# Low parts of the mixer's weights: made once and kept in DRAM

## The chip, the core and the metric

The kernel runs on one core of a Trainium2 chip. Its engines work side by side, each with its own queue of instructions taken in order: TensorE (PE) multiplies, VectorE (DVE), ScalarE (ACT) and GpSimd (POOL) work element by element, SyncE (SP) issues the DMAs here. The metric is device time of one execution in microseconds (us), as the median of several runs; less is better.

## The reference

One decoder layer on x of 2048 tokens by 1024 channels, all float32: a mixer of two groups of gated linear attention heads, then a squared-ReLU MLP, each between RMS norms. Cut to what matters here:

```python
def hybrid_mixer(h, w_in, w_gk_up, b_gk, gla_norm_w, hgrn_norm_w, lb, w_out):
    z = h @ w_in                     # 1024 x 3600
    gq, gk, gv, gg, glr, hq, hf, hi, hg = jnp.split(z, _split_points(), axis=-1)
    ...
    o_a = gated_head_norm(chunked_gated_linear_attention(q_a, k_a, v_a, log_a), gg, gla_norm_w)
    ...
    o_b = gated_head_norm(chunked_gated_linear_attention(q_b, k_b, v_b, jnp.log(f)), hg, hgrn_norm_w)
    return jnp.concatenate([o_a, o_b], axis=-1) @ w_out       # 1024 x 1024

h = x + rmsnorm(hybrid_mixer(rmsnorm(x, pre_mix_norm), w_in, ...), post_mix_norm)
u = rmsnorm(h, pre_mlp_norm) @ w_up
out = h + rmsnorm(jnp.square(jax.nn.relu(u)) @ w_down, post_mlp_norm)
```

## The kernel before

PE multiplies in a rounded float32 format. To keep precision each operand is written as a high part (the value rounded to that format, made by ACT) and a low part (value minus high part, made by DVE or POOL), and each product is three matmuls: high by high, high by low, low by high (`mm3`, L236 to 241). `split` (L224) makes the pair: L229 is ACT's copy, L230 the subtraction.

The mixer runs over four blocks of 512 tokens (`mixer`, L299). A block goes through four units of heads in the order 0, 2, 3, 1 and then the output projection `out_proj` (L700). A unit projects its query, key or gate channels (`zchan`, L427; weights stationary) and then its values and output gates (`values`, L443; activations stationary, four token tiles against eight pieces of weight). Unit 0 has 16 columns more and takes each piece in two matmuls of 272 and 256 columns. The attention itself is made of tasks that are advanced between these products (`tile_task`, L526; decays L565, scores L632, states L654, outputs L687).

The weights come as pieces of 128 x 512 (128 x 528 for the values of unit 0). `plan` (L271) lists 72 pieces for each block, the same 72 four times: 56 of `w_in` and 16 of `w_out`. Each names the engine of its subtraction: POOL for the channel pieces and every second value piece (40 of 72), DVE for the rest (32). The class `Weights` (L39) handles them: `load` (L53) issues the DMAs of a piece on SP (L64; one for a channel or `w_out` piece, two for a value piece, three in unit 0) into one of 4 raw buffers `wr`, up to four pieces ahead of the last one split; `prep` (L69) splits one; `pump` (L82) splits up to n more while fewer than 12 are live; `take` hands one to the products, `free` counts those that the products are done with. High and low parts share 24 buffers `w`. A raw buffer is free again when the subtraction has read it. So every block loads and splits all weights anew.

SP also issues all other transfers: x and its transpose, the residuals of the block before (`residual`, L772; L790, L801), and in block 3 the operands of the MLP's first product (`combine`, L807): its operands are loaded (L819), scaled by ACT, added by POOL and stored (L824), 16 loads and 28 stores for its first half. After the mixer come `up` and `down`, the two MLP products, which the change leaves alone. The order of instructions on each engine is set when the program is built, by a scheduler that goes by priority and by its own estimate of when things are ready.

Of the kernel before, what the change touches and what calls it, by code (L numbers as in the profile page):

```python
# [7 lines left out]
F32 = mybir.dt.float32  # L8
F32R = mybir.dt.float32r
I32 = mybir.dt.int32  # L10
AF = mybir.ActivationFunctionType
# [5 lines left out]
P = 128  # L17
# [9 lines left out]
NG = FF // P // GF  # L27
WM = 528
WS = 576
NFLAG = P * (2 * NCH + 1)  # L30
EPS = 1e-6
LIMIT = 64.0
# [6 lines left out]
class Weights:  # L39

    LIVE = 12
    RAW = 4

    def __init__(self, layer):
        self.layer, self.plan, self.raw, self.parts = layer, [], {}, {}
        self.loaded = self.split = self.taken = self.freed = 0

    def add(self, views, chan=False, eng="vector"):  # L50
        self.plan.append((views, chan, eng))

    def load(self):  # L53
        y = self.layer
        while self.loaded < len(self.plan) and self.loaded < self.split + self.RAW:
            views, chan, _ = self.plan[self.loaded]
            raw = y.wp.tile([P, WM], F32, tag="wr", name=y.name("wr"), bufs=self.RAW)
            at = 0
            for v in views:
                n = v.shape[-1] * (4 if chan else 1)  # L60
                dst = raw[:, at:at + n]
                if chan:
                    dst = dst.rearrange("p (k n) -> p k n", n=P)
                y.nc.sync.dma_start(dst, v)  # L64
                at += n
            self.raw[self.loaded] = raw[:, :at]
            self.loaded += 1

    def prep(self):  # L69
        self.load()  # L70
        y, i = self.layer, self.split
        raw = self.raw.pop(i)
        n = raw.shape[-1]
        hi, lo = (y.wp.tile([P, WS], F32R, tag="w", name=y.name("w"), bufs=2 * self.LIVE)[:, :n] for _ in range(2))
        y.split(hi, lo, raw, eng=getattr(y.nc, self.plan[i][2]))
        if self.plan[i][1]:
            hi, lo = (z.rearrange("p (k n) -> p k n", n=P) for z in (hi, lo))
        self.parts[i] = (hi, lo)
        self.split += 1
        self.load()  # L80

    def pump(self, n):  # L82
        while n and self.split < len(self.plan) and self.split - self.freed < self.LIVE:
            self.prep()
            n -= 1

    def take(self):
        if self.split == self.taken:
            assert self.split - self.freed < self.LIVE
            self.prep()  # L90
# [7 lines left out]
class Layer:  # L98
# [21 lines left out]
        self.hold = False  # L120
        self.rs, self.hn, self.vdone, self.vg = {}, {}, {}, {}

    def run(self, h1d, h2d, hcd, ud):
        tc = self.tc
        self.h1d, self.h2d, self.hcd, self.ud = h1d, h2d, hcd, ud
        with tc.tile_pool(name=f"ac{self.tag}", bufs=1, reuse_waits="tile") as self.ac:


            with ExitStack() as late:
                with ExitStack() as ctx:  # L130
                    self.sb = ctx.enter_context(tc.tile_pool(name=f"sb{self.tag}", bufs=1))
                    self.ps = ctx.enter_context(tc.tile_pool(name=f"ps{self.tag}", bufs=1, space=PSUM))
                    with ExitStack() as early:
                        self.wp = early.enter_context(tc.tile_pool(name=f"wp{self.tag}", bufs=1, side="right"))
                        self.pz = early.enter_context(
                            tc.tile_pool(name=f"pz{self.tag}", bufs=1, space=PSUM, side="right"))
                        self.plan()
                        self.mixer()
                    self.open_up(late)
                    self.drain()  # L140
                    if not self.exact:
                        self.judge()
                self.up()
            self.down()
# [125 lines left out]

    def plan(self):  # L271
        io = self.io
        self.w = Weights(self)

        def chan(src, cols):
            for half in range(2):
                for col in cols:
                    rows = src[half * 512:half * 512 + 512, col:col + P]
                    self.w.add([rows.rearrange("(k p) n -> p k n", p=P)], True, "gpsimd")

        for b in range(NBLK):
            for u in self.UNITS:
                if u < 2:
                    chan(io["w_in"], (GQ + u * P, GK + u * P))
                else:
                    for h in (2 * u - 4, 2 * u - 3):
                        chan(io["w_in"], (HF + h * P,))
                        chan(io["w_in"], (HQ + h * P,))
                for k in range(KT):
                    self.w.add([io["w_in"][k * P:(k + 1) * P, c0:c0 + n] for c0, n in self.value_cols(u)],  # L290
                               eng=("gpsimd", "vector")[k % 2])
            for half in range(2):
                for u in self.UNITS:
                    for k in (2 * u, 2 * u + 1):
                        self.w.add([io["w_out"][k * P:(k + 1) * P, half * 512:half * 512 + 512]])
# [1 line left out]


    def mixer(self):  # L299
        for tag, n, width in (("wr", Weights.RAW, WM), ("w", 2 * Weights.LIVE, WS), ("pad", 1, 48)):  # L300
            self.wp.tile([P, width], F32R if tag == "w" else F32, tag=tag, name=self.name(tag), bufs=n)
        self.drain(self.stats(0))
        self.load_const("ident")
        self.pre_mix = self.static("pre_mix_norm", [P, KT])
        self.hn[0] = []
        for _ in self.prepare(0, 4):
            pass
        self.setup_mixer()
        for b in range(NBLK):
            self.b, self.oT, self.g = b, {}, {}  # L310
            if b == NBLK - 1:
                self.pre_mlp = self.small("pre_mlp", [P, KT])
                self.nc.sync.dma_start(self.pre_mlp, self.io["pre_mlp_norm"])

                def halves():
                    wide = [self.t([P, D], "wide") for _ in range(2)]
                    return [w[:, h * 512:h * 512 + 512] for w in wide for h in range(2)]

                self.spawn(self.combine(0, halves))
            for u in self.UNITS:  # L320
                if u == 3 and b + 1 < NBLK:
                    self.spawn(self.stats(b + 1))
                self.hold = True
                self.unit(u)
                self.hold = False
                self.step()
            self.out_proj(b)
# [479 lines left out]
    def combine(self, s, new):  # L807
# [5 lines left out]
        for j in range(4):  # L813
# [9 lines left out]
            def keep(i, tile):  # L823
                nc.sync.dma_start(self.hcd[i, s, j], tile)  # L824

            a21, a22 = load(j, 1), load(j + 4, 1)
            yield
            keep(3, a22)
# [426 lines left out]
def build(tc, io, force=False):  # L1255
    nc = tc.nc
    nc.scalar.preload_act_table_set("natural_log_exp_and_others")
    with ExitStack() as ctx:
        ent = ctx.enter_context
        cp = ent(tc.tile_pool(name="consts", bufs=1))  # L1260
        dp = ent(tc.tile_pool(name="scratch", bufs=1, space=DRAM))
        c = {}

        def const(key, shape, val):
            c[key] = cp.tile(shape, F32, name=f"c_{key}")
            nc.vector.memset(c[key], val)

        c["ident"] = cp.tile([P, P], F32, name="c_ident")
        c["cmask"] = cp.tile([P, P], I32, name="c_cmask")
        const("ones", [P, P], 1.0)  # L1270
        const("neghalf", [P, NCH], -0.5)
        const("flag_a", [P, NCH], 0.0)
        const("flag_b", [P, NCH], 0.0)
        const("fmin", [P, 1], 1.0)
        c["verdict"] = cp.tile([1, 1], I32, name="c_verdict")
        h1d = dp.tile([T, D], F32, name="h1_scratch")
        h2d = dp.tile([D, T], F32, name="h2_scratch")
        hcd = dp.tile([7, T // TM, 4, P, TB], F32, name="h2_operands")
        ud = dp.tile([7, T // TM, NG, P, TB], F32, name="u_operands")

        fast = Layer(tc, io, c, False)
        fast.run(h1d, h2d, hcd, ud)

        ok = nc.values_load(c["verdict"][0:1, 0:1], min_val=0, max_val=NFLAG)
        with tc.If(ok < (NFLAG + 1 if force else NFLAG)):
            slow = Layer(tc, io, c, True)
            slow.run(h1d, h2d, hcd, ud)


_OUT = "out"  # L1290
# [51 lines left out]
```

## Time and profile before

| | before |
|---|---|
| median of 3 runs | 2339.5 us (2334.85 to 2341.5) |
| the profiled execution | 2335.3 us |
| its span, first to last instruction | 2333.4 us |
| PE, DVE, ACT, POOL busy | 96%, 65%, 50%, 33% |
| mean granted clock of PE | 0.985 |
| bytes moved by DMA | 343 MB, 147 GB/s on average |

The profile is of one execution. "Busy" is the share of the span in which an engine works on an instruction; PE's matmuls overlap. The granted clock of PE has two levels, full (1.00, 2.4 GHz) and half (1.2 GHz). "DMA share" is the mean busy share of the 16 DMA engines. A wait is named by what ended it: "PE zp_f L240 <- DVE w_f L230" is PE, standing before a matmul of line 240, until DVE's instruction of line 230 had finished.

### The profile page before, as it was taken

The page shows a single profiled execution, that of the slowest core. Times are in us where ns is not written, and L with a number is a line of the kernel's source. Part 1 is how long each engine was busy: PE and PEld are TensorE (multiplying, and loading weights), DVE is VectorE, ACT ScalarE, POOL GpSimd, SP SyncE. Part 2 cuts the span into 40 slices and gives each one's busy share as a digit, 9 for nine tenths or more (in the row PEclk, how much of TensorE's full clock was granted, in tenths as well). Part 3 has the DMA queues.
Part 4 walks back from the last instruction along what each step waited for, and adds up shares of the span by engine and source line. Part 5 has one row for each costly group of instructions (what it writes and reads, how often), then busy time and mean ns, then how long its engine had stood idle before and what let it go on. Part 6 is the DMA issues. An engine that isn't in the chain of part 4 may idle for free. (4 is left out here: it accounts for less than half of the span.)

```text
span 2333.4 us, 31583 instructions
## 1 busy us (share of the span) xinstructions
PE 2241.2 (96%) x10922; PEld 1846.3 (79%) x10922; DVE 1517.6 (65%) x2368; ACT 1170.8 (50%) x2268; POOL 778.2 (33%) x537
## 2 busy tenths in 40 slices
PE   7999999999999889998999999999899999999995
PEld 6788878888788868876888878888788878888884
DVE  4675566555763676657775687655636776777687
ACT  5764566556654566455555565555543322333242
POOL 4330323124321543124532333333312332233265
PEclk9999999999999989999999999999999999999998
DMA  6322652246324752359744464444444433344265
GB/s 183 114 78 73 182 163 73 71 132 187 98 75 123 247 174 73 99 176 292 241 174 151 155 229 176 153 151 155 146 167 126 136 115 111 127 136 132 94 203 195
DMA packets 294762, 343.42 MB, mean 147 GB/s; under 512 B 25776, under 2 KB 214464, under 8 KB 294592
## 3 DMA queue, kind: packets, MB, share of 16 engines
q1 hardware_dynamic: 294592, 341.30, 45.5%
q8 instruction: 88, 1.44, 0.3%
q14 instruction: 82, 0.67, 0.1%
HBM read 242.65 MB, written 98.57 MB: 146 GB/s over the span
## 5 line engine op out<-in xcount | busy, mean ns | idle before, releaser
L239 PE MATMUL zp_f<-w_f,act_f 128*128 128x512 f32 (+2 forms) x896 | 329.8, 369 | 3.3 <-ACT ct_f L408 1.9
L240 PE MATMUL zp_f<-w_f,act_f 128*128 128x512 f32 (+2 forms) x896 | 326.0, 364 | 6.3 <-DVE w_f L230 4.5
L241 PE MATMUL zp_f<-w_f,act_f 128*128 128x512 f32 (+2 forms) x896 | 324.2, 364 | 0.0
L230 POOL TENSOR_TENSOR w_f<-wr_f,w_f 128x512 fp32r<-128x512 f32 (+1 forms) x160 | 220.8, 1391 | 285.0 <-ACT w_f L229 265.5
L868 ACT ACTIVATE u_f<-raw_f 128x1024 fp32r<-128x1024 f32 x111 | 117.7, 1061 | 332.3 <-PE Y_f L1195 223.8
L229 ACT ACTIVATE w_f<-wr_f 128x512 fp32r<-128x512 f32 (+1 forms) x288 | 177.6, 629 | 138.9 <-DMA wr_f<-in_w_in 68.1
L862 POOL TENSOR_TENSOR u_f<-raw_f,u_f 128x1024 fp32r<-128x1024 f32 x55 | 135.4, 2463 | 302.4 <-ACT u_f L868 302.3
L248 POOL TENSOR_TENSOR rs_f<-ms_f,c_neghalf 128x1 f32<-128x1 f32 (+1 forms) x80 | 66.5, 838 | 434.0 <-DVE ms_f L246 433.9
L240 PEld LDWEIGHTS zp_f<-w_f,act_f 128*128 128x128 f32 x896 | 169.6, 189 | 31.2 <-DVE w_f L230 5.1
L239 PEld LDWEIGHTS zp_f<-w_f,act_f 128*128 128x128 f32 x896 | 169.4, 189 | 31.6 <-issue 3.1
L241 PEld LDWEIGHTS zp_f<-w_f,act_f 128*128 128x128 f32 x896 | 169.6, 189 | 25.1 <-issue 0.7
L1194 PE MATMUL Y_f<-act_f,u_f 128*128 128x512 f32 x384 | 150.4, 395 | 11.7 <-DVE acc_f L1153 10.4
L239 PE MATMUL zp_f<-act_f,w_f 128*128 128x512 f32 x384 | 153.4, 403 | 3.1 <-ACT act_f L229 3.1
L240 PE MATMUL zp_f<-act_f,w_f 128*128 128x512 f32 x384 | 152.7, 398 | 1.8 <-DVE act_f L230 1.8
L241 PE MATMUL zp_f<-act_f,w_f 128*128 128x512 f32 x384 | 152.7, 398 | 0.0
L1153 DVE TENSOR_TENSOR acc_f<-acc_f,Y_f 128x1024 f32<-128x1024 f32 (+1 forms) x89 | 107.1, 1204 | 68.5 <-PE Y_f L1196 67.4
L1195 PE MATMUL Y_f<-act_f,u_f 128*128 128x512 f32 x384 | 151.0, 393 | 0.0
L1196 PE MATMUL Y_f<-act_f,u_f 128*128 128x512 f32 x384 | 150.3, 393 | 0.1
L230 DVE TENSOR_TENSOR w_f<-wr_f,w_f 128x512 fp32r<-128x512 f32 (+1 forms) x128 | 102.4, 813 | 67.6 <-ACT w_f L229 63.0
L868 ACT ACTIVATE w_f<-t_f 128x512 fp32r<-128x512 f32 x128 | 79.9, 628 | 112.5 <-PE Y_f L977 52.0
L865 DVE TENSOR_TENSOR w_f<-t_f,w_f 128x512 fp32r<-128x512 f32 x98 | 84.6, 863 | 42.5 <-ACT w_f L868 42.4
L862 POOL TENSOR_TENSOR ev_f<-ev_f,ev_f 128x512 f32<-128x512 f32 x40 | 63.2, 1579 | 141.3 <-ACT ev_f L995 73.3
(241 smaller groups left out, 5880.7 us busy)
## 6 DMA issues: line engine op xcount, KB each, us to landing
u_operands<-ev_f SPq DMA_DIRECT2D x224, 256.0 KB, 2.1
raw_f<-u_operands SPq DMA_DIRECT2D x222, 256.0 KB, 3.0
wr_f<-in_w_in SPq DMA_DIRECT2D x256, 128.0 KB, 2.5
wr_f<-in_w_up SPq DMA_DIRECT2D x64, 512.0 KB, 3.8
wr_f<-in_w_in SPq DMA_DIRECT2D x96, 256.0 KB, 3.1
wide_f<-in_x SPq DMA_DIRECT2D x32, 512.0 KB, 6.1
wr_f<-in_w_out SPq DMA_DIRECT2D x64, 256.0 KB, 3.0
wr_f<-in_w_down SPq DMA_DIRECT2D x32, 512.0 KB, 4.7
```

The source lines that it names most:

```text
L229: nc.scalar.activation(hi, raw, AF.Copy)
L230: eng.tensor_sub(lo, raw, hi.bitcast(F32))
L239: mm(out, a[0], b[0], start=i == 0, stop=False)
L240: mm(out, a[0], b[1], start=False, stop=False)
L241: mm(out, a[1], b[0], start=False, stop=i == n - 1)
L862: nc.gpsimd.tensor_tensor(out, a, b, op)
L865: nc.vector.tensor_tensor(out, a, b, op)
L868: self.nc.scalar.activation(hi, raw, AF.Copy)
L1153: nc.vector.tensor_add(a[:, x], a[:, x], z[:, x])
L1194: mm(zx, hi[:, k, tok], whi, start=not loaded and k == 0, stop=False, skip_group_check=loaded)
L1195: mm(zx, hi[:, k, tok], wlo, start=False, stop=False, skip_group_check=loaded)
L1196: mm(zx, lo[:, k, tok], whi, start=False, stop=k == 1, skip_group_check=loaded)
```

## The change

In block 0 each piece is split as before, and then its low part is stored to a DRAM tensor `w_low` with one slot for each of the 72 pieces. In blocks 1 to 3 `load` fetches the low part from there, right after the raw piece, and `prep` only lets ACT make the high part. The 24 shared buffers become 12 for high parts (`w`) and 12 for low parts (`wl`). For these pieces `load` stops at 12 pieces ahead of the last one freed. Since `w_low` is passed to both layers that the program holds, `run` and the constructor of `Weights` have one more argument.

```diff
+PIECES = 72
...
+    def part(self, tag, n):
+        y = self.layer
+        return y.wp.tile([P, WS], F32R, tag=tag, name=y.name(tag), bufs=self.LIVE)[:, :n]
 
     def load(self):
         y = self.layer
         while self.loaded < len(self.plan) and self.loaded < self.split + self.RAW:
-            views, chan, _ = self.plan[self.loaded]
+            i, kept = self.loaded, self.loaded >= PIECES
+            if kept and i >= self.freed + self.LIVE:
+                return
+            views, chan, _ = self.plan[i]
...
-            self.raw[self.loaded] = raw[:, :at]
+            self.raw[i] = raw[:, :at]
+            if kept:
+                self.lo[i] = self.part("wl", at)
+                y.nc.sync.dma_start(self.lo[i].bitcast(F32), self.low[i % PIECES, :, :at])
             self.loaded += 1
 
     def prep(self):
...
-        hi, lo = (y.wp.tile([P, WS], F32R, tag="w", name=y.name("w"), bufs=2 * self.LIVE)[:, :n] for _ in range(2))
-        y.split(hi, lo, raw, eng=getattr(y.nc, self.plan[i][2]))
+        hi = self.part("w", n)
+        if i in self.lo:
+            lo = self.lo.pop(i)
+            y.nc.scalar.activation(hi, raw, AF.Copy)
+        else:
+            lo = self.part("wl", n)
+            y.split(hi, lo, raw, eng=getattr(y.nc, self.plan[i][2]))
+            y.nc.sync.dma_start(self.low[i, :, :n], lo.bitcast(F32))
...
+        wlow = dp.tile([PIECES, P, WM], F32, name="w_low")
```

## Rows read from the trace of the kernel before

**Rows 1.** Page, busy us, share of the span and instructions of each engine.

```profile
PE 2241.2 (96%) x10922; PEld 1846.3 (79%) x10922; DVE 1517.6 (65%) x2368; ACT 1170.8 (50%) x2268; POOL 778.2 (33%) x537
```

**Rows 2.** Windows, blocks 0 to 3: busy us, PEclk, DMA share, GB/s.

```profile
0.00:262.00 262.00, 244.73 (x1343) 202.75 (x1344) 153.54 (x372) 150.80 (x352) 76.77 (x65) 0.99 0.42 120
262.00:514.00 252.00, 247.26 (x1393) 206.08 (x1392) 154.17 (x355) 147.94 (x352) 69.96 (x60) 1.00 0.40 118
514.00:765.00 251.00, 245.97 (x1388) 205.02 (x1387) 151.84 (x349) 150.57 (x356) 74.00 (x63) 1.00 0.41 126
765.00:1035.00 270.00, 257.57 (x1403) 213.59 (x1402) 166.21 (x357) 153.56 (x362) 85.57 (x71) 0.96 0.45 139
```

**Rows 3.** Waits of PE, 262 to 760 us: us in total, times, longest.

```profile
PE at_f L663 <- ACT ct_f L651: 3.1, 2, 1.5
PE at_f L639 <- DVE ct_f L594: 2.5, 2, 1.6
PE zp_f L240 <- DVE w_f L230: 2.3, 2, 1.7
```

**Rows 4.** Waits of PE, 760 to 1030 us.

```profile
PE at_f L639 <- DVE ct_f L594: 3.9, 1, 3.9
PE at_f L649 <- DVE ct_f L593: 2.2, 1, 2.2
PE zp_f L240 <- DVE w_f L230: 2.1, 1, 2.1
PE at_f L797 <- DVE wide_f L791: 2.0, 1, 2.0
PE zp_f L240 <- POOL w_f L230: 1.8, 1, 1.8
PE zp_f L239 <- ACT w_f L229: 0.4, 1, 0.4
```

**Rows 5.** Page, groups: the subtractions of the weights (busy, mean ns, idle before).

```profile
L230 POOL TENSOR_TENSOR w_f<-wr_f,w_f 128x512 fp32r<-128x512 f32 (+1 forms) x160 | 220.8, 1391 | 285.0 <-ACT w_f L229 265.5
L230 DVE TENSOR_TENSOR w_f<-wr_f,w_f 128x512 fp32r<-128x512 f32 (+1 forms) x128 | 102.4, 813 | 67.6 <-ACT w_f L229 63.0
```

**Rows 6.** Windows, stretches about the start of block 3, columns as rows 2.

```profile
750.00:760.00 10.00, 10.00 (x49) 8.34 (x48) 4.22 (x8) 7.23 (x16) 0.00 (x0) 1.00 1.01 346
...
790.00:840.00 50.00, 47.98 (x291) 42.28 (x291) 21.55 (x37) 34.73 (x70) 26.01 (x22) 0.96 0.97 300
840.00:870.00 30.00, 23.95 (x127) 17.98 (x125) 27.41 (x65) 16.30 (x34) 10.10 (x7) 0.77 0.36 106
```

**Rows 7.** One line, the scan of the decays: ns min/median/max, first and last start.

```profile
L571 DVE TENSOR_TENSOR_SCAN ct_f<-c_ones,ct_f x96: 389/399/1509, 70.9 to 958.6; 128x128 f32<-128x128 f32 x96
```

**Rows 8.** Timeline, block 3: start us, us, engine and line.

```profile
833.05 1.74 POOL L832 TENSOR_TENSOR wide_f<-wide_f 128x512 f32<-128x512 f32 x1
...
833.68 4.45 DVE L571 TENSOR_TENSOR_SCAN ct_f<-c_ones,ct_f 128x128 f32<-128x128 f32 x4
```

**Rows 9.** Waits of SP's queue, 262 to 1030 us.

```profile
SPq L64 <- POOL w_f L230: 236.7, 82, 24.8
```

**Rows 10.** One line, the loads of raw pieces: ns min/median/max of an issue; landing.

```profile
L64 SPq DMA_DIRECT2D wr_f<-in_w_in x384: 327/379/1650, 7.3 to 941.2; - x192
...
DMA to landing us min/median/max: 1.8/2.8/6.8
```

**Rows 11.** Timeline of PE, block 0 at the first values.

```profile
35.44 0.39 PE L239 MATMUL zp_f<-w_f,act_f 128*128 128x272 f32 x1 [0.98 <-ACT w_f L229]
```

**Rows 12.** Windows, the start of block 0, columns as rows 2.

```profile
14.00:44.00 30.00, 26.41 (x146) 22.92 (x147) 18.04 (x28) 16.46 (x32) 19.83 (x12) 1.00 0.73 189
```

**Rows 13.** Timeline of SP, block 3: the loads of sixteen pieces, first and last.

```profile
818.67 3.10 SPq L64 DMA_DIRECT2D wr_f<-in_w_in  x4
...
831.30 4.93 SPq L64 DMA_DIRECT2D wr_f<-in_w_in  x8
```

**Rows 14.** Waits of ACT, 760 to 1030 us.

```profile
ACT w_f L229 <- DMA wr_f<-in_w_in: 15.0, 12, 3.0
```

More of the change, by code (lines that the diff above doesn't have):

```diff
@@ L44, with __init__ @@
     RAW = 4
-    def __init__(self, layer):
+    def __init__(self, layer, low):
         self.layer, self.plan, self.raw, self.parts = layer, [], {}, {}
+        self.low, self.lo = low, {}
         self.loaded = self.split = self.taken = self.freed = 0
@@ L121, in __init__, with run @@
         self.rs, self.hn, self.vdone, self.vg = {}, {}, {}, {}
-    def run(self, h1d, h2d, hcd, ud):
+    def run(self, wlow, h1d, h2d, hcd, ud):
         tc = self.tc
-        self.h1d, self.h2d, self.hcd, self.ud = h1d, h2d, hcd, ud
+        self.wlow, self.h1d, self.h2d, self.hcd, self.ud = wlow, h1d, h2d, hcd, ud
         with tc.tile_pool(name=f"ac{self.tag}", bufs=1, reuse_waits="tile") as self.ac:
@@ L272, in plan @@
         io = self.io
-        self.w = Weights(self)
+        self.w = Weights(self, self.wlow)
         def chan(src, cols):
@@ L299, in mixer @@
     def mixer(self):
-        for tag, n, width in (("wr", Weights.RAW, WM), ("w", 2 * Weights.LIVE, WS), ("pad", 1, 48)):
-            self.wp.tile([P, width], F32R if tag == "w" else F32, tag=tag, name=self.name(tag), bufs=n)
+        for tag, n, width in (("wr", Weights.RAW, WM), ("w", Weights.LIVE, WS), ("wl", Weights.LIVE, WS), ("pad", 1, 48)):
+            self.wp.tile([P, width], F32R if tag in ("w", "wl") else F32, tag=tag, name=self.name(tag), bufs=n)
         self.drain(self.stats(0))
@@ L1281, in build @@
         fast = Layer(tc, io, c, False)
-        fast.run(h1d, h2d, hcd, ud)
+        fast.run(wlow, h1d, h2d, hcd, ud)
         ok = nc.values_load(c["verdict"][0:1, 0:1], min_val=0, max_val=NFLAG)
@@ L1286, in build @@
             slow = Layer(tc, io, c, True)
-            slow.run(h1d, h2d, hcd, ud)
+            slow.run(wlow, h1d, h2d, hcd, ud)
 _OUT = "out"
```

## The prediction

> **What bounds the kernel now.** I read the page first: the tensor engine (PE) is busy 2241.2 of 2333.4 us, VectorE (DVE) 65%, ScalarE (ACT) 50%, GpSimd (POOL) 33% [rows 1]. So this change, which takes work from DVE and POOL, can only pay where PE stands still for them or runs at the lower clock. The mixer fills the first 1035 us, so I cut it into its four token blocks with the windows view [rows 2]. In blocks 1, 2 and 3, the only ones that lose work, PE is idle 252 - 247.3 = 4.7, 251 - 246.0 = 5.0 and 270 - 257.6 = 12.4 us, 22.1 us together. Blocks 1 and 2 run at clock 1.00, block 3 at 0.96, which is 0.04 x 270 = 10.8 us lost. The whole purse is therefore about 33 us, 1.4% of the time, however many instructions go.
>
> Who holds that purse is in the waits of PE. In blocks 1 and 2 it waits 2.3 us for a low part (L240), 2.5 for the product at L594 and 3.1 for a copy at L651 [rows 3]; with 1.9 us for ScalarE's evacuation of a projection these are all of the idle time there. In block 3 it waits 2.1 + 1.8 us for low parts, 0.4 for a high part, 3.9 and 2.2 for the products at L594 and L593, 2.0 for a residual [rows 4]. So low parts as such cost PE 2.3 + 2.1 + 1.8 = 6.2 us; the attention's products on DVE cost 2.5 + 3.9 + 2.2 = 8.6 us.
>
> **What is removed.** 40 of the 72 pieces of a block are split on POOL, 32 on DVE. Three blocks lose 120 POOL subtractions of 1391 ns = 167 us and 96 on DVE of 813 ns = 78 us [rows 5]. Nearly all of that lies beside PE's work.
>
> (a) *Waits for low parts, 6.2 us.* They stand at the first values of a block (unit 0), where eight pieces are used up in 8 x 3 matmuls of 272 columns, faster than they can be made. After the change the low part comes by DMA, and the next one late is the high part on ACT, the same 0.6 us copy, for which PE waits 0.4 us today [rows 4], or the load. SyncE now has four issues per such piece, not three: 8 x 0.38 = 3 us more of its time in each burst [rows 10]; in return the raw buffer is free after ACT's copy, not after the subtraction, and SyncE waits 237 us for POOL's subtractions alone in blocks 1 to 3 [rows 9]. Bounds: -6.2 (all gone) to +9 (SyncE's issues set the burst, three times). I take two thirds of the gain, -4, because the row on SyncE shows that it waits more than it issues.
>
> (b) *Waits for attention products, 8.6 us.* Here POOL's instructions lengthen DVE's. The scan at L571 takes 389 ns at best, 399 in the median and 1509 at worst [rows 7]; four of them take 4.45 us beside a POOL instruction of 1.74 us and the next one behind it [rows 8], near 1.1 us each. From 840 to 870 us DVE is busy 27.4 of 30 us while POOL works 10.1 [rows 6]; PE waits its 3.9 and 2.2 us there. Bounds: -8.6 to 0; I take a third, -3, since the other POOL work of block 3 (the sums of `combine`) stays and, by (e), slides towards this place.
> The Trainium skill (SBUF — State Buffer, "Who interferes with whom") says that a DVE instruction with two SBUF inputs contends with a GpSimd instruction that reads SBUF, and that whoever comes second is blocked for the whole of the other. The trace agrees as far as 1509 - 389 ns is most of a POOL subtraction. By that rule alone all of (b) would go, and the sum would be 5.6 us lower.
>
> (c) *Clock.* Block 3 lies at 0.96; 840 to 870 us alone at 0.77, 0.23 x 30 = 6.9 us lost right after the two long waits of (b) [rows 6]. Bounds -10.8 to +6.9 (one more such stretch); I take -2, as the lost stretches lie behind idle gaps of which I let a part go.
>
> **What is added.** 72 stores in block 0 and 216 loads in blocks 1 to 3, all on SyncE's queue; a block's low parts are 64 x 262,144 + 8 x 270,336 bytes = 18.9 MB.
>
> (d) *Block 0.* A store waits for its low part, and the loads behind it on SyncE wait. But the next raw load waits for the same subtraction already, since it reuses the raw buffer which that one reads; so the wait is not new, only the issue of 0.33 to 0.38 us is [rows 10]. The low buffer is used again only twelve pieces later, so nobody waits for the landing. Where it hurts is the start, before pieces are made ahead: at 35.4 us PE stands 0.98 us for ACT's copy of a value piece [rows 11]. Eight value pieces, each 0.38 us later, are 3 us, with no cover left there. Bounds: 0 (PE has the next matmuls of other pieces) to +6 (the DMA engines are also 0.73 busy from 14 to 44 us [rows 12], 22 of 30 us, and some 16 stores of 0.76 us add 12). I take +3.
>
> (e) *The DMA engines in blocks 1 to 3.* At full share they move 346 GB/s [rows 6], so a low part costs 0.76 us and a block's 55 us, 0.22 of its 250 us on top of 0.40 to 0.45 [rows 2]. That is free except from 790 to 840 us in block 3, where the share is 0.97 [rows 6] because `combine(0)` moves 44 tiles beside the residuals. Sixteen pieces are loaded in that stretch, one DMA each, in runs of 4, 4 and 8 from 818.7 to 836.2 us [rows 13], so 16 x 0.76 = 12 us come on top of 48.5: 11 us must slide behind 840, where the share is 0.36 and there is room. Weights are made up to twelve pieces ahead, and a piece of this kind lasts 12 matmuls, near 2.7 us, so PE has some 30 us of slack for a late piece; what has none is ACT, which takes its copies in order and already waits 15.0 us for raw pieces in block 3 [rows 14]. Bounds 0 to +11; I take +2, nearer the lower end because PE was busy 48.0 of those 50 us under the full queue.
>
> (f) *Order.* The new gate in `load` (a piece at most twelve ahead of the last one freed) takes away the raw load four ahead where twelve pieces are live: in unit 0 the loads of the four pieces after its values now stand behind the values, not among them. Landing takes 2.8 us in the median and 6.8 at worst [rows 10], and ACT's copy now stands closer behind its load. ACT is idle 252 - 148 = 104 us in block 1 [rows 2]; I put this at nothing, the cover being that idle time; without it each block would show a few waits of 2.8 us on ACT, which PE sees only when its PSUM buffers for projections (four) are all waiting to be copied out. A low load also waits until PE has done with the buffer's former piece, twelve before; behind it queue raw loads and the residuals' transfers. SyncE stands in such waits today, by way of the subtraction that itself waits for PE; I put it at nothing, and the bound is within (e).
>
> **Sum.** -4 - 3 - 2 + 3 + 2 = -4 us. The profiled execution took 2335.3 us, its span 2333.4 with 1.9 around it; it would become 2331. The median of the three runs, 2339.5, stands 4.2 above that execution, so I forecast 2335.5 - rounded, 2335, no difference that can be told: about 0.3%, 7 us, is what a measurement of this kernel can tell from no change.
>
> **Rivals.** *DVE set free.* (a), (b) and (c) are paid out nearly whole: -6 - 8 - 8 + 3 + 2 = -17, 2322. For it: the 1509 ns scans, and that block 3's clock loss stands behind waits of this kind. Against it: in blocks 1 and 2 only 2.5 us wait on those products, and the 3.1 us for L651 are a chain of PE and ACT with neither DVE nor POOL in it. This is also where the skill's rule on the shared port leads.
>
> *Full DMA queue in block 3, slower.* The 11 us that slide out of 790 to 840 us are met by ACT, in order, at raw pieces and at the operands of `combine`; PE's projections then find no free PSUM buffer. It decides once the slide is longer than what those buffers and the twelve pieces hide. Price: up to 11 us of PE idle, and a clock stretch like that of 840 to 870 us behind it, 6.9 us, plus 3 in block 0, less 4 of (a): +17, 2356; from +8 on if the slide is half hidden. For it: a share of 0.97, and four waits of 2 to 4 us in block 3 already. Against it: PE hardly idled in that very stretch.
>
> *Nothing but block 0's price.* The waits keep their size because ACT's copy or the load takes the place of the subtraction: +3, 2342.
>
> **How the numbers follow.** Forecast (2328 to 2343) 0.45; DVE set free (2314 to 2328) 0.25; full queue (above 2343) 0.25; block 0's price alone 0.05. Faster by over 0.3%: the second case and a quarter of the first, 0.36. Slower: the third and a little of the first, 0.27. Within 0.3%: 0.37. The range of 8 in 10 reaches into both: 2318 to 2352; it leaves out the lower end of the second case and the upper half of the third. The forecast's own range is 2328 to 2343.
>
> **What would show it.** In the profile after: no subtraction for weights in blocks 1 to 3, DVE about 78 and POOL about 167 us less. (a) No wait of PE at L240 for DVE or POOL from 262 us on; a wait for a DMA there means that the load took over. (b) The scan's longest times gone in blocks 1 and 2, and waits at L639 below 2.5 us in 262 to 760. (c) A granted clock above 0.96 in block 3. (d) PE's first value matmuls up to 3 us later, block 0 longer by as much and no more. (e) Share at 1.0 for some 60 us from 790 on, with PE still above 0.95 busy. The forecast is wrong if ACT's wait for raw pieces in block 3 doubles and PE's idle time there grows with it, or if block 0 grows by more than 6 us.

## The result, and the profile after

The changed kernel takes 2314.15 us in the median (2310.13 to 2317.83), the kernel before 2340.4 in the same comparison (2334.85 to 2341.66): ratio 0.9892, 95% interval 0.9874 to 0.991, 26 us less. The forecast was 2335, with 2318 as its lower end.

The page of the changed kernel, its engines:

```profile
PE 2232.5 (96%) x10922; PEld 1841.4 (80%) x10922; DVE 1414.5 (61%) x2272; ACT 1172.0 (51%) x2268; POOL 613.5 (26%) x417
```

Against [rows 1] DVE has 103 us less and POOL 165. DVE's 96 subtractions were 78 us of it [rows 5]; the other 25 us are its remaining instructions, which have become shorter. The same windows as [rows 2], cut where the blocks of this trace end (busy of PE, PEld, DVE, ACT, POOL, then granted clock, DMA share, GB/s):

```profile
0.00:262.00 262.00, 242.11 (x1334) 200.32 (x1335) 154.43 (x374) 151.54 (x354) 69.81 (x61) 1.00 0.62 197
262.00:514.00 252.00, 252.00 (x1409) 210.41 (x1408) 120.83 (x325) 150.52 (x358) 18.16 (x21) 0.99 0.63 197
514.00:758.00 244.00, 243.13 (x1367) 202.66 (x1367) 113.37 (x311) 145.33 (x347) 15.27 (x20) 0.99 0.62 195
758.00:1015.00 257.00, 251.41 (x1414) 209.64 (x1413) 134.43 (x326) 156.23 (x365) 40.77 (x37) 1.00 0.68 222
```

PE now idles 0.0, 0.9 and 5.6 us in blocks 1 to 3, where it idled 4.7, 5.0 and 12.4; in block 0 it idles 19.9 us where it idled 17.3 (most of both is the start). That is 39.4 against 26.4 us up to the end of the mixer. The clock is 0.99, 1.00, 1.00, 0.96 before (2.6 + 10.8 = 13.4 us lost) and 1.00, 0.99, 0.99, 1.00 after (2.5 + 2.4 = 4.9). Together 13.0 + 8.5 = 21.5 us; the clocks have two digits, so that each loss is good to about 1 us.

Marks on ACT show the same by block: the copy of a block's first query projection (L408, now L427) in blocks 1, 2, 3 and the last square of the output projection (L714, now L733), from the timeline. Before:

```profile
285.44 0.59 ACT L408 ACTIVATE ct_f<-zp_f 128x512 f32<-128x512 f32 x1
537.33 0.59 ACT L408 ACTIVATE ct_f<-zp_f 128x512 f32<-128x512 f32 x1
791.71 0.59 ACT L408 ACTIVATE ct_f<-zp_f 128x512 f32<-128x512 f32 x1
1034.77 0.59 ACT L714 ACTIVATE ct_f<-zp_f 128x512 f32<-128x512 f32 x1
```

After:

```profile
284.00 0.59 ACT L427 ACTIVATE ct_f<-zp_f 128x512 f32<-128x512 f32 x1
533.14 0.59 ACT L427 ACTIVATE ct_f<-zp_f 128x512 f32<-128x512 f32 x1
783.05 0.59 ACT L427 ACTIVATE ct_f<-zp_f 128x512 f32<-128x512 f32 x1
1014.82 0.59 ACT L733 ACTIVATE ct_f<-zp_f 128x512 f32<-128x512 f32 x1
```

From mark to mark the kernel gains 1.4, 2.8, 4.5 and 11.3 us, 20.0 in all; what follows the mixer takes 1298.6 us before and 1301.2 after, so 2.6 are given back there. The spans of these two executions differ by 17.4 us, the medians by 26.2: the profiled execution of before was 5.1 us under its median, that of after 3.7 above its own. I explain the 20.0 us of the traces and leave that scatter alone.

The waits of PE that [rows 3] and [rows 4] show are nearly gone. After, 262 to 760 us:

```profile
PE zp_f L258 <- ACT ct_f L427: 0.6, 1, 0.6
PE at_f L816 <- DVE wide_f L810: 0.3, 1, 0.3
```

and 760 to 1016 us:

```profile
PE at_f L816 <- DVE wide_f L810: 2.1, 1, 2.1
PE at_f L713 <- DVE ct_f L701: 1.7, 1, 1.7
PE zp_f L258 <- ACT w_f L90: 1.0, 1, 1.0
PE zp_f L258 <- ACT ct_f L427: 0.7, 1, 0.7
```

No wait for a low part is left, none for the products of the attention where they stood before (L639, L649), and none for the copy at L651, which I had called a chain without DVE or POOL. One wait of 1.7 us for DVE stands at another step of the attention (L713, L694 before). The two stretches of [rows 6]:

```profile
790.00:840.00 50.00, 47.85 (x303) 40.28 (x303) 28.69 (x62) 37.25 (x76) 11.65 (x10) 1.00 1.02 343
840.00:870.00 30.00, 28.26 (x170) 22.38 (x169) 22.25 (x54) 20.86 (x56) 8.40 (x7) 1.00 0.75 242
```

The DMA engines are full from 790 to 840 us and busy to 0.75 behind, as forecast; PE is as busy as before in the first stretch and gains 4.3 us of work and the clock in the second. What did grow is landing: page of after, part 6 (KB of one, us from issue to landing), where a value load took 2.5 and a channel load 3.1 us on the page of before:

```profile
wl_f<-w_low SPq DMA_DIRECT2D x192, 256.0 KB, 4.1
wr_f<-in_w_in SPq DMA_DIRECT2D x256, 128.0 KB, 3.7
...
wr_f<-in_w_in SPq DMA_DIRECT2D x96, 256.0 KB, 4.8
```

### The profile page after: what moved, and what is told of

Its sections match the earlier page's. It is cut to its first block, busy times and chain, and to the rows that moved or that the text cites. A ratio compares the mean times of both kernels' runs of the same rounds, so it can differ in the third digit from the quotient of the medians.

```text
span 2316.0 us, 31617 instructions
## 1 busy us (share of the span) xinstructions
PE 2232.5 (96%) x10922; PEld 1841.4 (80%) x10922; DVE 1414.5 (61%) x2272; ACT 1172.0 (51%) x2268; POOL 613.5 (26%) x417
## 5 line engine op out<-in xcount | busy, mean ns | idle before, releaser
L258 PE MATMUL zp_f<-w_f,act_f 128*128 128x512 f32 (+2 forms) x896 | 327.9, 367 | 6.7 <-ACT ct_f L733 2.2
L259 PE MATMUL zp_f<-wl_f,act_f 128*128 128x512 f32 (+2 forms) x896 | 323.3, 361 | 0.0
L260 PE MATMUL zp_f<-w_f,act_f 128*128 128x512 f32 (+2 forms) x896 | 322.1, 362 | 0.0
L258 PEld LDWEIGHTS zp_f<-w_f,act_f 128*128 128x128 f32 x896 | 168.0, 188 | 34.2 <-issue 2.9
L90 ACT ACTIVATE w_f<-wr_f 128x512 fp32r<-128x512 f32 (+1 forms) x216 | 132.9, 631 | 118.9 <-DMA wr_f<-in_w_in 68.3
L260 PEld LDWEIGHTS zp_f<-w_f,act_f 128*128 128x128 f32 x896 | 168.2, 188 | 25.6 <-issue 0.5
L259 PEld LDWEIGHTS zp_f<-wl_f,act_f 128*128 128x128 f32 x896 | 168.3, 188 | 23.9 <-issue 0.2
L1213 PE MATMUL Y_f<-act_f,u_f 128*128 128x512 f32 x384 | 150.6, 396 | 12.5 <-DVE acc_f L1172 10.5
L258 PE MATMUL zp_f<-act_f,w_f 128*128 128x512 f32 x384 | 154.2, 405 | 2.8 <-ACT act_f L248 2.8
L259 PE MATMUL zp_f<-act_f,w_f 128*128 128x512 f32 x384 | 153.2, 399 | 2.1 <-DVE act_f L249 2.1
L260 PE MATMUL zp_f<-act_f,wl_f 128*128 128x512 f32 x384 | 153.3, 399 | 0.0
L996 PE MATMUL Z_f<-a_f,w_f 128*128 128x512 f32 x256 | 101.2, 396 | 4.6 <-POOL a_f L881 3.0
L1010 DVE TENSOR_TENSOR ev_f<-Y_f,p_f 128x512 f32<-128x512 f32 x96 | 66.0, 688 | 64.7 <-PE Y_f L997 64.7
L995 PE MATMUL Z_f<-a_f,w_f 128*128 128x512 f32 x256 | 100.6, 394 | 3.5 <-DVE ev_f L1010 2.1
```

Source lines behind the costliest of these rows:

```text
L90: y.nc.scalar.activation(hi, raw, AF.Copy)
L258: mm(out, a[0], b[0], start=i == 0, stop=False)
L259: mm(out, a[0], b[1], start=False, stop=False)
L260: mm(out, a[1], b[0], start=False, stop=i == n - 1)
L995: mm(z, whi[:, k, :], hi, start=first and k == 0, stop=False, skip_group_check=more)
L996: mm(z, whi[:, k, :], lo, start=False, stop=False, skip_group_check=more)
```

## The experiments

The theory after the result: the gain is *relief*, DVE and POOL free of the subtractions; PE waited for what they made late. Rivals: *readiness* (the low part is there when its load lands, and raw buffers come free earlier), and within relief the question whose work it is that costs, DVE's or POOL's. Ratios are to the kernel before, run beside; the changed kernel stands at 0.9892.

| run | what differs | median us | ratio, 95% interval |
|---|---|---|---|
| e1_subtract_anyway | change, all subtractions made, unread | 2340.05 | 1.0004 (0.9994 to 1.0014) |
| e2_only_pool_pieces | change for POOL's 40 pieces | 2315.62 | 0.9897 (0.9879 to 0.9915) |
| e3_only_dve_pieces | change for DVE's 32 pieces | 2327.97 | 0.9962 (0.9937 to 0.9986) |
| e4_high_too | high and low parts kept | 2321.33 | 0.9925 (0.9908 to 0.9943) |
| e10_pool_idle_work | change, POOL subtracts beside, bound to nothing | 2325.44 | 0.9942 (0.9922 to 0.9962) |
| e13_pool_in_place | change, POOL subtracts in the raw buffer, unread | 2329.82 | 0.9963 (0.9949 to 0.9977) |
| e7_all_on_dve | before, all subtractions on DVE | 2314.56 | 0.9892 (0.9871 to 0.9914) |
| e16_all_and_sums_on_dve | e7, and combine's sums on DVE | 2306.48 | 0.9858 (0.984 to 0.9875) |
| e17_change_no_pool | change, and nothing of weights or combine on POOL | 2314.27 | 0.9905 (0.9882 to 0.9927) |
| e11_block0_on_dve | change, block 0 on DVE | 2317.65 | 0.991 (0.9893 to 0.9926) |
| e12_high_too_dve | e4, block 0 on DVE | 2319.78 | 0.9918 (0.9902 to 0.9935) |
| e15_dve_and_block3 | e7, low parts loaded in block 3 | 2316.29 | 0.9908 (0.9889 to 0.9927) |
| e6_block3_only | change for block 3 alone | 2329.08 | 0.9963 (0.9951 to 0.9976) |
| e5_stores_only | block 0's stores alone | 2335.45 | 0.9988 (0.9977 to 1.0) |
| e9_gate_only | buffers and gate alone | 2342.75 | 1.0015 (1.0005 to 1.0025) |
| e8_low_twice | change, low parts loaded twice | 2337.36 | 0.9984 (0.997 to 0.9998) |
| e14_load_and_dve | change, low parts made again on DVE | 2328.15 | 0.9958 (0.9941 to 0.9974) |
| e18_spare_transfers | e7, 216 transfers nobody reads | 2369.97 | 1.0141 (1.0118 to 1.0163) |

**Relief or readiness.** e1 keeps everything of the change, the early low parts too, and gives DVE and POOL their subtractions back:

```diff
         if i in self.lo:
             lo = self.lo.pop(i)
             y.nc.scalar.activation(hi, raw, AF.Copy)
+            getattr(y.nc, self.plan[i][2]).tensor_sub(raw, raw, hi.bitcast(F32))
```

> The changed kernel, but in blocks 1 to 3 the subtraction is still made on its old engine, in place on the raw buffer, and nothing reads the result; the products use the loaded low part. Theory 'relief' (the gain is DVE and POOL being free of 245 us of subtractions): the gain goes, ratio 0.998 to 1.002 to the kernel before, and waits at the products of the attention (L639, L649, L663 of the kernel before, 11.7 us in all) are back. Rival 'readiness' (the gain is that the low part is there when its load lands, without two engines in a row): ratio stays near 0.989, only these waits come back in part.

The whole gain went. Its waits of PE, 262 to 760 us:

```profile
PE at_f L659 <- DVE ct_f L614: 3.8, 2, 2.8
PE zp_f L259 <- ACT ct_f L428: 3.2, 1, 3.2
PE at_f L683 <- ACT ct_f L671: 1.9, 2, 1.3
PE at_f L669 <- DVE c_fmin L544: 0.9, 1, 0.9
```

L659, L669 and L683 are L639, L649 and L663 of the kernel before: the attention's waits are back, that for ACT's copy among them, while no product waits for a low part. Low parts that are ready early are therefore not enough for the gain. One thing e1 also puts back is the hold on the raw buffer; that is taken up below.

**Whose work.** e2 and e3 keep the parts of one engine only (`kept = i >= PIECES and self.plan[i][2] == "gpsimd"`, or `"vector"`).

> Only the 40 pieces of a block whose subtraction is POOL's are kept in DRAM and loaded; the 32 of DVE are split in every block as before. If POOL's instructions were what lengthened DVE's work (shared access to SBUF): at least three quarters of the gain, ratio 0.989 to 0.992. If DVE's own 78 us were what mattered: a quarter or less, 0.997. If readiness in the bursts of unit 0 is what matters (four pieces of each engine there): about half, 0.994 to 0.995.

> The mirror: only the 32 pieces whose subtraction is DVE's are kept and loaded; the 40 of POOL are split in every block as before. POOL in the way of DVE: a quarter of the gain or less, ratio 0.997 to 0.999. DVE's own time: most of it, 0.990 to 0.992. Readiness in the bursts: about half, 0.994 to 0.995.

POOL's pieces alone give 0.9897, all of the change within the intervals; DVE's alone 0.9962, about a third. With POOL out, DVE's subtractions cost nothing that can be told. By their medians the two add up to more than the change, though the intervals leave room for a plain sum. e7 goes further and needs no DRAM at all:

```diff
-        y.split(hi, lo, raw, eng=getattr(y.nc, self.plan[i][2]))
+        y.split(hi, lo, raw)
```

> The kernel before, all its weight subtractions on DVE, none on POOL, no DRAM. POOL in the way of DVE: faster, 0.990 to 0.996, though DVE has 160 more subtractions of near 0.69 us = 110 us more. DVE's own time as the bound of the attention: slower, 1.005 to 1.02.

It gives the same ratio as the change, 0.9892, with DVE busier, not freer: 168 us in block 1 where the kernel before has 154 [rows 2]. Windows of e7:

```profile
0.00:262.00 262.00, 248.87 (x1369) 206.52 (x1370) 172.41 (x428) 156.68 (x365) 15.03 (x23) 1.00 0.42 122
262.00:514.00 252.00, 252.00 (x1415) 210.35 (x1415) 167.80 (x402) 151.76 (x358) 17.86 (x22) 1.00 0.41 123
514.00:762.00 248.00, 248.00 (x1398) 207.01 (x1398) 166.08 (x391) 150.17 (x355) 22.36 (x24) 1.00 0.43 130
762.00:1020.00 258.00, 248.93 (x1378) 206.41 (x1377) 169.30 (x384) 152.14 (x361) 38.70 (x35) 0.97 0.49 152
```

PE does not idle in blocks 1 and 2, and block 0, where the change leaves POOL's work alone, gains too: its mark falls from 285.4 to 276.5 us. The mark overstates it somewhat, as PE has 1453 instructions ahead of it in e7 and 1466 in the kernel before; PE's idle time up to the mark falls from 18.2 to 13.1 us, and its clock is 1.00 where it was 0.99. So DVE's total time was not the bound: what counted was how long POOL's instructions made DVE's.

**By what POOL costs.** e10 lets POOL work without anyone depending on it, e13 in the raw buffer, which comes free only behind it:

```diff
+            if self.plan[i][2] == "gpsimd":
+                junk = y.wp.tile([P, WS], F32R, tag="j", name=y.name("junk"), bufs=1)[:, :n]
+                y.nc.gpsimd.tensor_sub(junk, hi.bitcast(F32), hi.bitcast(F32))
```

```diff
+            if self.plan[i][2] == "gpsimd":
+                y.nc.gpsimd.tensor_sub(raw, raw, hi.bitcast(F32))
```

> The changed kernel, and in blocks 1 to 3 POOL makes its 40 subtractions a block on the finished high part alone, into a buffer nobody reads; no raw buffer, no product and no DMA waits for them (weight buffers are 544 wide, not 576, to make room). If POOL's instructions as such lengthen DVE's, which they run beside: three quarters of the gain or more goes, 0.997 to 1.000. If the gain was that raw buffers come free earlier, or that low parts come earlier: ratio stays at 0.989 to 0.991.

> The changed kernel; in blocks 1 to 3 POOL still makes its 40 subtractions a block, in place on the raw buffer (which therefore comes free only behind it), nobody reads them; DVE makes none. If running beside DVE is all that POOL does: as e10_pool_idle_work, 0.993 to 0.995. If holding the raw buffer is the other half: 0.998 to 1.000, as e1_subtract_anyway, whose DVE subtractions then cost nothing.

By the times alone, half of the gain goes with work that nothing waits for (0.9942) and about two thirds with the work in the raw buffer (0.9963). The windows from the start to the mixer's end, with columns as before, say something else. The changed kernel, e10 and e13:

```profile
0.00:1014.82 1014.82, 988.48 (x5519) 822.85 (x5520) 522.87 (x1332) 603.43 (x1422) 144.01 (x138) 1.00 0.64 203
0.00:1025.32 1025.32, 999.28 (x5519) 822.30 (x5520) 546.18 (x1332) 603.37 (x1421) 275.20 (x258) 1.00 0.63 201
0.00:1027.04 1027.04, 993.74 (x5519) 825.48 (x5520) 564.41 (x1332) 603.92 (x1421) 303.49 (x258) 0.99 0.63 201
```

DVE makes the same 1332 instructions in all three. They take 23 us longer in e10 and 42 us longer in e13, so POOL's work lengthens DVE's even where neither waits for the other's result.

What this costs PE is shown by e13 alone: PE idles 33.3 us there and 26.3 in the changed kernel, and the clock falls to 0.99. In e10 PE idles 26.0 us at a clock of 1.00, no more than in the changed kernel. The 10.5 us by which its mixer ends later are busy time of PE, for the same 5519 instructions. They go with the other part of its edit, the weight buffers that are 544 wide: the matmuls of 512 columns take 393 ns in the median, not 389, in block 0 too, where POOL's work is the same. In the changed kernel and in e10 (ns min/median/max):

```profile
L258 PE MATMUL zp_f<-act_f,w_f x384: 387/389/792, 15.1 to 936.6; 128*128 128x512 f32 x192
L261 PE MATMUL zp_f<-act_f,w_f x384: 387/393/793, 14.9 to 946.1; 128*128 128x512 f32 x192
```

So e10's time is no evidence of what POOL's presence costs, and a slower PE may have hidden some of that cost. Its instruction is also lighter, 1101 ns on average against 1353 in e13, as it reads one buffer twice.

In e13, whose matmuls have the old 389 ns, the raw buffer is held longer, and SyncE waits 63 us for it behind POOL. But ACT does not wait longer for raw pieces. The changed kernel, then e13, 262 to 1020 us:

```profile
ACT w_f L90 <- DMA wr_f<-in_w_in: 64.8, 57, 4.0
ACT w_f L90 <- DMA wr_f<-in_w_out: 15.6, 14, 2.4
```

```profile
ACT w_f L90 <- DMA wr_f<-in_w_in: 60.2, 51, 3.6
ACT w_f L90 <- DMA wr_f<-in_w_out: 16.5, 13, 2.3
```

In e1 these are 61.4 and 17.9 us, so late raw pieces are not the cause there either. Whether SyncE's standing reaches PE by another way is not shown; PE's wait for the residuals (L818, L816 in the changed kernel) is 4.8 us in e13 and 2.1 in the changed kernel. From e13 to e1 the last third of the gain goes when DVE has its subtractions as well.

The scan of the decays shows the lengthening itself (ns min/median/max). In the changed kernel, where POOL still subtracts in block 0 and adds in `combine`:

```profile
L590 DVE TENSOR_TENSOR_SCAN ct_f<-c_ones,ct_f x96: 391/400/1453, 73.1 to 938.2; 128x128 f32<-128x128 f32 x96
```

and in e16, where POOL has neither:

```profile
L571 DVE TENSOR_TENSOR_SCAN ct_f<-c_ones,ct_f x96: 390/399/425, 67.2 to 925.4; 128x128 f32<-128x128 f32 x96
```

The longest scan falls from 1509 [rows 7] to 425 ns. The Trainium skill's rule (SBUF — State Buffer, "Who interferes with whom": a DVE instruction with two SBUF inputs contends with a GpSimd instruction that reads SBUF, and the second one is blocked for the whole of the first) agrees with this, in size too: 1509 - 389 = 1120 ns is most of a subtraction of 1391.

**A version that beats both.** e16 moves the sums as well (in `combine`, for its first half, `eng = nc.vector`), e17 does so in the changed kernel with block 0's subtractions on DVE:

> The kernel before with all weight subtractions on DVE and the 16 sums of combine in block 3 as well, so that POOL has only the small reciprocal roots in the mixer. POOL in DVE's way in block 3 too: 0.985 to 0.988. DVE then the bound in block 3 (169 of 258 us busy in e7 already): 0.989 to 0.993.

> The changed kernel with block 0's subtractions and the 16 sums of combine on DVE: POOL has neither in the mixer, and DVE has none of the weights in blocks 1 to 3. If DVE's freed time is worth something once POOL is out of its way: 0.983 to 0.985. If it is worth nothing and only the traffic is left of the change: 0.987 to 0.990, worse than e16_all_and_sums_on_dve at 0.9858.

e16 is the fastest kernel of the study, 0.9858; its interval just touches those of the change and of e7. Windows of e16 and e17 up to the mixer's end:

```profile
0.00:1000.84 1000.84, 984.99 (x5519) 820.03 (x5520) 662.79 (x1604) 600.27 (x1421) 64.07 (x82) 1.00 0.43 130
0.00:1006.53 1006.53, 987.60 (x5519) 821.58 (x5520) 531.17 (x1388) 603.00 (x1422) 65.07 (x82) 1.00 0.64 205
```

Once POOL is out of the way, keeping low parts in DRAM is a loss: e17 is at 0.9905, and the intervals do not meet. Its mixer ends 5.7 us later though DVE is 132 us less busy; 3.1 us of that are idle time of PE. By the marks, e17 against e16: block 0 is 5.1 us longer (281.6 against 276.5; PE idles 16.4 us in it, not 12.5), which the stores and their buffers account for; block 1 is 2.9 and block 2 2.2 longer, block 3, with `combine`'s sums on DVE, 4.5 shorter (229.6 against 234.1). The last three lean on where the mark falls: in e17 PE has 13 and 11 more of its instructions in blocks 1 and 2 and 16 fewer in block 3. PE's idle time in block 3 is 2.2 us against 3.4, and 0.4 against 0.0 in blocks 1 and 2 together. So what DVE's freed time gives back, with the loads in place, is about 1 us in block 3.

e11 and e12 put block 0's subtractions on DVE in the change and in e4; e15 is e7 with stores in block 1 and loads in block 3 alone.

> The changed kernel with block 0's subtractions all on DVE, so that POOL makes none in any block. By the theory that POOL's subtractions are what costs: block 0 gains as well, 2 to 5 us, ratio 0.987 to 0.988. If block 0 has nothing to gain (it waited 0.6 and 1.5 us for attention steps) or DVE becomes its bound: 0.989 to 0.991.

> All subtractions on DVE in blocks 0 to 2, the low parts stored in block 1 and loaded in block 3 alone, where combine is. By the marks: block 0 and 1 as in e7_all_on_dve (276 and 246 us, less if the stores in block 1 cost up to 6), block 3 as in the changed kernel (232 against 235): 0.985 to 0.988. If block 3 needs no relief of DVE, or the stores cost what block 3 gains: 0.989 to 0.991.

e11 gains nothing (0.991): with stores, block 0's mark only falls from 284.0 to 282.6 us, where e7 without stores has 276.5. e15 (0.9908) gains nothing on e7 either.

e4 stores pairs of high and low part as one transfer and loads them as one, without raw pieces and copies in blocks 1 to 3.

> Block 0 stores high and low part of a piece in one transfer of 512 KB, blocks 1 to 3 load the pair in one, with no raw piece and no copy on ACT (216 copies of 0.63 us less, same bytes in blocks 1 to 3, 19 MB more stored in block 0). If what is left in blocks 1 to 3 hangs on ACT's copies or on SyncE's issues: another 3 to 8 us, ratio 0.986. If they are hidden already (PE idle 0.0 and 0.9 us in blocks 1 and 2 of the changed kernel): as the changed kernel, 0.989, or up to 5 us worse if the second store of a piece delays the first loads of block 0.

> High and low parts kept as pairs, as in e4_high_too, and block 0's subtractions all on DVE. If e4's loss against the changed kernel came from its 38 MB of stores at the start of block 0, which stay: 0.991 to 0.993. If it came from POOL in block 0: 0.987 to 0.989.

e4 is 0.9925, 7 us behind the change. Its window up to the mixer's end, and the line of its matmuls that was shown for e10:

```profile
0.00:1016.58 1016.58, 998.08 (x5519) 820.53 (x5520) 521.87 (x1332) 490.26 (x1206) 142.74 (x138) 1.00 0.64 221
L261 PE MATMUL zp_f<-act_f,w_f x384: 388/394/796, 15.2 to 936.6; 128*128 128x512 f32 x192
```

PE idles 18.5 us where it idles 26.3 in the changed kernel, but it is busy 9.6 us longer for the same instructions: with each pair in one buffer its matmuls take 394 ns in the median. What e4 saves in waits it loses in matmuls, and whether ACT's copies cost anything it cannot show. Moving block 0 off POOL (e12, 0.9918) changes nothing that can be told; its matmuls are as long (392 ns on this line).

**The parts of the change that cost.** e5, e9 and e6 do one part alone:

> Block 0 stores its 72 low parts (12 and 12 buffers), but blocks 1 to 3 load nothing and split as before: the price of the stores alone. By the forecast +3 us, 1.0013; by the trace of the changed kernel, where block 0 is not longer, 0 us, 1.000.

> The buffers and the gate of the changed kernel (12 and 12, a piece at most 12 ahead of the last one freed in blocks 1 to 3), with the subtractions of the kernel before and no DRAM. If part of the gain is a better order of loads: 0.995 to 0.998. If the gate costs ACT waits for raw pieces that PE sees: 1.002 to 1.006. If it does neither: 1.000.

> Block 0 stores, only block 3 loads its low parts, blocks 1 and 2 split as before. From the marks of the two traces block 3 holds 11 of the 20 us gained up to the mixer's end, blocks 1 and 2 the rest: ratio 0.994 to 0.996. If the blocks' gains hang together (a late block 2 makes block 3 worse): 0.997 or more.

Stores alone: 0.9988, no loss that can be told. Gate and buffers: 1.0015, 3.5 us of loss. Block 3 alone: 0.9963, a third of the gain, where the marks had given it half. In its trace block 3 gains 9.9 of those 11.3 us, and blocks 1 and 2, which split as before, are 3.7 us longer than in the kernel before; single traces scatter by as much, so how the rest of the gain divides is not shown.

**Traffic, three tries.** e8 issues each low load twice, e14 makes the loaded part again on DVE, e18 adds a transfer from x to a spare place in DRAM for each piece to e7.

> The changed kernel with every low part loaded twice into its buffer: 57 MB more by DMA in blocks 1 to 3, 216 more issues. If the DMA engines have slack, as the forecast took it outside one stretch of 50 us: 0.989 to 0.992. If the full queue at the start of block 3 bites (share 1.02 from 790 to 840 us in the changed kernel): 0.995 or more, with waits of PE behind late loads there.

> Stores and loads of the changed kernel, but the low part is then made anew on DVE over the loaded one, in all blocks; POOL makes none. Against e7_all_on_dve (0.9892, same subtractions, no DMA): if the added DMA is hidden, 0.989 to 0.991; if the change pays for its DMA, 0.993 or more.

> The kernel before with all weight subtractions on DVE (e7_all_on_dve, 0.9892), and with each piece of blocks 1 to 3 one more transfer of the same size, from x to a spare place in DRAM, that no engine waits for: 57 MB read and written again, 216 issues. If the change's traffic is hidden in itself: 0.988 to 0.991. If traffic alone delays raw pieces and what hangs on them: 0.993 or more.

None prices the traffic alone. In e8 SyncE stood 90.6 us for the first of two loads into the same buffer, and PE 11.7 us for low parts (waits, 262 to 1030 us):

```profile
SPq L80 <- DMA wl_f<-w_low: 90.6, 123, 4.0
```

```profile
PE zp_f L260 <- DMA wl_f<-w_low: 11.7, 7, 2.9
```

In e14 DVE stood 60.3 us for the loads. In e18 the spare transfers, bound to nothing, were all placed in block 0, whose DMA engines were full and whose PE idled 51 us:

```profile
0.00:262.00 262.00, 211.34 (x1135) 172.59 (x1135) 137.03 (x358) 121.98 (x288) 10.71 (x18) 0.93 0.98 296
```

A full queue can stop PE, as over block 0 in e18, but it need not. From 790 to 840 us, e8 and then e14:

```profile
790.00:840.00 50.00, 44.58 (x264) 38.87 (x263) 14.06 (x30) 26.76 (x57) 9.57 (x9) 0.97 1.06 374
790.00:840.00 50.00, 50.00 (x322) 43.28 (x321) 32.52 (x73) 37.98 (x79) 11.46 (x10) 1.00 1.04 353
```

The best price for the change's own traffic, buffers and order is the pair e16 and e17: 5.7 us at the mixer's end of these traces, 7.8 by the medians.

## Why the prediction was wrong

The views were the right ones: the purse of 33 us in blocks 1 to 3 was there, and 22 us of it were paid. What failed is how much of it I let each term have.

(b), the attention's products, is the step that failed. I took a third of 8.6 us and nothing of the 3.1 at L651. Everything but 1.7 us of waits of this kind went, the 3.1 too: -10.0 us where I took -3. The row of the 1509 ns scan and the Trainium skill's rule on the shared access said so, and I set them aside with the argument that `combine`'s sums would slide into the place of the subtractions. They did slide (five of the sixteen lie between 842 and 850 us, where one lay before), and by the medians of e7 and e16 they cost 8 us, in intervals that just touch; but they are 16 instructions in one block, the subtractions 120 in three. And a copy on ACT that waits behind a chain of DVE work is not free of DVE because neither end of its wait names it: e1 brought it back together with the others.

(c), the clock. Block 3's 10.8 us came back whole, and blocks 1 and 2 lost 4.9 to single stretches at the lower level, where block 0 lost none: 8.5 us net against the 2 that I took. For the 6.9 us of the stretch from 840 to 870 us this goes with (b): the lower level had stood behind the waits of 3.9 and 2.2 us, and both are gone. What the short stretches follow is not shown; those after the change stand in blocks where PE hardly idles.

(a), waits for low parts: 6.2 us before, and 1.0 after, which is for a high part, as I had thought; -5.2 where I took -4, the right size. But the early load is not needed for it: e7, which makes the low part on DVE in 0.69 us, has 0.7 us of such waits. And e1, which has no such wait, gains nothing in all.

(d), block 0, forecast +3: PE's idle time there grew by 2.6 us, while its mark came 1.4 us earlier: it lost no clock, and PE had 1450 instructions ahead of the mark, not 1466. In a block 0 that POOL doesn't hold back, stores and buffers cost 5.1 us by the mark, 3.9 of it idle time (e17 against e16); I had 3.

(e) and (f): the slide of about 11 us out of the full stretch came, PE stayed at 47.85 of 50 us, as argued. Slower landing reached ACT: its waits for `in_w_in` pieces from 262 us to the mixer's end are 64.8 us where they were 48.1, and PE didn't see them. The gate, put at nothing, costs 3.5 us together with the divided buffers (e9).

The sum of -4 became -21.5 in idle and clock: (b) and (c) hold 7.0 and 6.5 of the 17.5 us that were missing, (e), which cost PE nothing that shows, 2 and (a) 1.2. The likeliest case should have been the rival "DVE set free", priced at -17 with a chance of 0.25; even its lower end, 2314, is where the median fell. What I had not looked at is block 0: I counted the purse only where work is removed, though POOL's subtractions cost time there too: 5.1 us of idle time of PE and some clock, 9 us by the mark (e7).

## What to carry to other kernels

Work handed to POOL to spare DVE was not spared here: DVE's instructions beside POOL's took longer, a scan by up to 1120 ns. So read the longest duration of a short DVE instruction against its median before giving POOL anything in a stretch whose chain runs through DVE. When a change removes work from two engines, first try to move it between them: here a change of one argument gave what 76 MB of traffic gave, and removing POOL's sums as well gave a third more. A wait that names neither of the engines in question can still be theirs, one link further back. And before the time of an experiment is put down to what it was made for, compare PE's busy time for the same instructions: e10 and e4 also changed the width or grouping of the weight buffers, and with that went matmuls 4 to 5 ns longer, some 10 us in all.

## What was not expected of the hardware

A single scan of 128 x 128 took 1509 ns at worst beside POOL and 425 without it, at the same median of 399. Loads of the same size landed in 4.8 us at a DMA share of 0.62 to 0.68 in the blocks and in 3.1 at 0.40 to 0.45. And 57 MB of copies from DRAM to DRAM at a share of 0.98 cost the kernel 55 us (e18 against e7), though no engine waited for them. In the three kernels whose weight buffers are 544 wide or hold pairs (e10, e4, e12), matmuls of 512 columns took 392 to 394 ns in the median, on the line shown, and 389 in the kernel before and in the changed one; what in the layout does it, no run shows.
